# Stick-breaking by summation by parts in a one-layer decoder trunk, and four rearrangements around it

## The chip, the core and the metric

The kernel runs on one core of a Trainium2 chip. Times are device microseconds of one execution. Five engines each work through a list of instructions of their own in order: TensorE (PE; its weight loads, PEld, overlap the matmuls), VectorE (DVE), ScalarE (ACT), GpSimd (POOL) and SyncE (SP, which only issues DMAs; ACT and POOL issue some too). An instruction that waits for a semaphore holds up all that stands behind it on its engine.

## What is computed

One layer of a hybrid trunk on 1024 tokens of width 1024 in fp32. One projection `h @ w_in` feeds three branches and their gates: an RWKV-7 recurrence (8 heads of 64), stick-breaking attention (8 heads of 64) and cross-attention to 256 memory tokens. The gated branches are summed, projected and added to x, and a convolutional feed-forward network follows. The part that the change rewrites is this:

```python
z = jnp.einsum('bhqd,bhkd->bhqk', qb, kb).astype(jnp.float32) * scale
mask = s_idx[None, :] < t_idx[:, None]
log_1mb = jnp.where(mask, jax.nn.log_sigmoid(-z), 0.0)
log_between = lax.cumsum(log_1mb, axis=3, reverse=True) - log_1mb
attn = jnp.where(mask, jnp.exp(jax.nn.log_sigmoid(z) + log_between), 0.0)
outs.append(jnp.einsum('bhqk,bhkd->bhqd', attn.astype(v.dtype), vb))
```

With `sn = sigmoid(-z)` (1 where masked) and the suffix products `P[s] = sn[s] * sn[s+1] * ... * sn[W-1]`, `P[W] = 1`, a weight is `attn[s] = sigmoid(z[s]) * P[s+1]`. Since `sigmoid(z) = 1 - sn`, that is also `P[s+1] - P[s]`, and the sum over s can be taken by parts: `sum attn[s] v[s] = v[W-1] + sum P[s] (v[s-1] - v[s])`, with `v[-1] = 0`.

## The kernel before

Every fp32 matmul operand is split into a high and a low part; a product is three matmuls, high by high, high by low and low by high. `split_w` (L84) loads a 512 KB weight tile on SP's queue into one of two "wr" buffers, copies the high part on ScalarE (L80) and subtracts on GpSimd (L81). `proj_item` (L664) is a projection: 8 k-steps of six matmuls of 512 columns, 48 in all, each k-step followed by a yield; `gate_item` (L703) is one for a gate, which is then multiplied by the row norm, passed through a sigmoid and stored to `gsd` or kept.

Work is woven by hand. `run` (L1668) makes a list `items` of such generators; `stream` starts the next one, which issues its weight load and split, before it runs the present one. `weave(main, filler, ratio)` advances a main generator and, after each of its yields, the filler `pump` by `ratio` yields on average. `pump` also advances the generator `inverse` by `pace` tenths of a step per yield. Matmuls, transposes and some VectorE instructions are pinned to program order; other instructions, DMAs included, are ordered by a scheduler when the program is built, from its own estimate of when they are ready.

In order of time:

- The items project r, k and v of the recurrence, woven with `rwkv_prep` (L308). Then come eight items of `sb_v` (L615): the value projection of stick-breaking in two groups (jg) of four, 24 matmuls an item. In the fourth item of a group ScalarE copies the four results, scaled, into `self.v` (L643), four tiles of [128 keys, 2 x 512] that the attention reads later.
- `rwkv_prep` writes each head's 64 x 64 chunk matrices to `mad`, and GpSimd loads them into `inst`, one matrix per partition. `inverse` (L459) inverts all 128 in place: 62 pairs of a product and an addition on VectorE (L466, L468), 124 steps, and then sixteen DMAs on GpSimd's queue to `td` (L475).
- `sb_attn` (L785) runs 64 units (pair of heads, half, head, block of 128 queries), with gates, memory projections and inverse steps as filler. `front` makes z in PSUM and two sigmoids, `sn` (L806) and `sp` (L807); `weigh` a reversed scan of products over `sn` (L813) and a multiply into `sp` (L814); `mid` transposes `sp` (L105, by way of L824) and copies it back from PSUM into the tile of `sn` (L825); `back` multiplies it by `self.v` and copies the sum into the one "ys" buffer (L845), from where ScalarE's queue stores it to `yd` (L848). These tiles are "at" tiles, of which there are seven. In program order a unit's `mid` comes two units after its `front`, its `back` four.
- `mem_attn` (L1001) does cross-attention; `back` copies y into the "ys" buffer (L1050) and stores it (L1051).
- `ld1` loads the stick-breaking result of `yd` (L1082) and splits it on ScalarE (L1073) and VectorE (L1074); the high part, `yhi`, takes the buffer of `inst`. The products with `w_br` follow in `branch_item` (L1090), as filler of `stage2` (L477), the recurrence over 16 chunks. Its loads are made in `load` (L490): chunk matrices `scr` (L493), values `vd` (L497) and inverses `td` (L498). Then come `group_norm` (L588), the last branch, the output projection and the feed-forward network.

`need(name)` advances the filler until an item has set that mark.

Of the kernel before, what the change touches and what calls it, by code (L numbers as in the profile page):

```python
# [22 lines left out]
NG = NC // 2  # L23
# [26 lines left out]
class Trunk:  # L50
# [408 lines left out]
    def inverse(self):  # L459
# [11 lines left out]
        for p in range(4):  # L471
            for h2 in range(2):
                for cc in range(2):
                    i0 = p * 32 + h2 * 16 + cc
                    nc.gpsimd.dma_start(self.td[p // 2, :, h2, :, p % 2, cc * 64 : cc * 64 + 64], X[i0 : i0 + 15 : 2])  # L475

    def stage2(self):  # L477
# [12 lines left out]
        def load(g, p, what="LV"):  # L490
# [3 lines left out]
            if "V" in what and p % 2 == 0:  # L494
# [3 lines left out]
                nc.sync.dma_start(V2[:, 512:768], self.td[p // 2, g].rearrange("h s p i -> (h s) (p i)"))  # L498
# [116 lines left out]
    def sb_v(self):  # L615
        nc = self.nc
        out = {}
        self.v = []

        def item(jg, kt):  # L620
# [4 lines left out]
            if (jg, kt) == (0, 3):  # L625
                self.v += [self.t4("A", n=1024) for _ in range(4)]

# [7 lines left out]
            for i in range(4):  # L635
# [5 lines left out]
                if kt == 3:  # L641
                    jj = jg * 4 + i
                    nc.scalar.activation(self.v[jj // 2][:, (jj % 2) * 512 : (jj % 2 + 1) * 512], out[jg][i], AF.Copy, scale=self.rsc[:, jj : jj + 1])  # L643
# [4 lines left out]
        return [item(jg, kt) for jg in range(2) for kt in range(4)]  # L648

    def head_norm(self, pst, nh, width, fold, neg=None):  # L650
# [8 lines left out]
        if neg is not None:  # L659
            nc.gpsimd.tensor_tensor(v3(neg), v3(f), b3(self.rscn), ALU.mult)  # L660
        nc.gpsimd.tensor_tensor(v3(f), v3(f), b3(self.rsc), ALU.mult)
# [61 lines left out]
    def sb_qk(self, p, out):  # L723
# [40 lines left out]
        def q_split(i):  # L764
# [7 lines left out]
            if i == 1:  # L772
                out.extend((st["S"], *st["K"], *st["f"]))

        def q_ss():
            nf = self.small("nf", [128, 16])
            f = self.head_norm(self.head_ss(st["q"][0]), 2, SBD, SBD ** -0.5, nf)
            st["f"] = f, nf
# [6 lines left out]
    def sb_attn(self, qk, need):  # L785
# [4 lines left out]
        def front(u):  # L790
            p, half, h2, b = units[u]
            need(f"sb{p}")
            S, K, KL, f, nf = qk[p]
            W = (b + 1) * 128
            ts = slice(b * 128, (b + 1) * 128)
            sn, sp = self.t4("at", n=1024), self.t4("at", n=1024)
            for w0 in range(0, W, 512):
# [9 lines left out]
                nc.scalar.activation(sp[:, w0:w1], pz[:, : w1 - w0], AF.Sigmoid, scale=f[:, i : i + 1])  # L807
            st[u] = (sn, sp)

        def weigh(u):  # L810
            W = (units[u][3] + 1) * 128
            sn, sp = st[u]
            self.pinned(nc.vector.tensor_tensor_scan(sn[:, :W][:, ::-1], sn[:, :W][:, ::-1], sp[:, :W], 1.0, ALU.mult, ALU.bypass))  # L813
            self.pinned(nc.vector.tensor_tensor(sp[:, : W - 1], sp[:, : W - 1], sn[:, 1:W], ALU.mult))  # L814

        def mid(u):
            b = units[u][3]
            W = (b + 1) * 128
            at, sp = st[u]
            for w0 in range(0, W, 512):  # L820
                w1 = min(w0 + 512, W)
                pt = self.ps("g")
                for o in range(w0, w1, 128):
                    self.transpose(pt[:, o - w0 : o - w0 + 128], sp[:, o : o + 128])  # L824
                nc.scalar.activation(at[:, w0:w1], pt[:, : w1 - w0], AF.Copy)  # L825

        def back(u):
            p, half, h2, b = units[u]
            ats = [st.pop(u + i)[0] for i in range(2)]
# [171 lines left out]
    def mem_attn(self, mq, need):  # L1001
# [666 lines left out]
    def run(self):  # L1668
# [36 lines left out]
        items += [lambda: drain(inv), ld1, gate(), mark("y1"), *br1, ld2, gate(), *br2]  # L1705
# [22 lines left out]
        pace[0] = 5  # L1728
        self.weave(self.sb_attn(qk, need), pump, 1.03, 0)
        pace[0] = 5  # L1730
# [6 lines left out]
        self.weave(st2, pump, 2.25, 0)  # L1737
# [82 lines left out]
```

## Time and profile before

| | us |
|---|---|
| three timed runs | 1930.93, 1934.08, 1934.30 (median 1934.08) |
| the profiled execution | 1926.05 |
| its span, first to last instruction | 1924.3 |
| mean granted TensorE clock in it | 0.985 |

The stages touched by the change lie in it as follows: value projection of stick-breaking about 240 to 287 us, stick-breaking attention 340 to 680, memory attention to about 818, start of branch 1 and of the recurrence 818 to 860, recurrence and branch products to about 1100. From 1311 on TensorE is all but full.

How to read the rows: in a table of stages each engine's busy time stands in us with its count of instructions, then the granted clock, the mean busy share of the 16 DMA engines, and GB/s. In a list of waits a row gives who waited, for whom, the sum in us, how often, and the longest. In a timeline a row is start, length, engine, line, operation, output <- input, and in brackets the idle time just before it and what ended it. A group row ends with count, busy us, mean ns, and the idle time before it. A DMA row gives count, size, and the median us from issue to landing.

### The profile page before, as it was taken

Reading aid. Unit: us, or ns where it says so; the run is one execution under the profiler, and the core shown is the slowest. Engines: PE = TensorE matmul, PEld = TensorE weight load, DVE = VectorE, ACT = ScalarE, POOL = GpSimd, SP = SyncE. Lnnn points to the kernel's source line nnn. Section 1 sums busy time; section 2 is a strip of 40 time slices with the busy share of each in tenths; the row PEclk is TensorE's granted clock in tenths of the full one; section 3 lists DMA queues with packets and bytes.
Section 4 is the critical chain, followed back from the end, with each engine's and each line's share of the span. In section 5 each row is a group of like instructions: output and inputs, shape, how many; then the busy total and the mean of one; then the engine's idle time right before and its main releaser. Section 6 shows DMA issues by size and latency. Waiting matters only on the chain. (4 is left out here: it accounts for less than half of the span.)

```text
span 1924.3 us, 27682 instructions
## 1 busy us (share of the span) xinstructions
PE 1834.8 (95%) x10500; PEld 1455.7 (76%) x10500; DVE 1230.2 (64%) x1702; ACT 922.4 (48%) x1729; POOL 791.7 (41%) x451
## 2 busy tenths in 40 slices
PE   8999999999998999979999989989999999999999
PEld 6777778777776787757777867767888888878877
DVE  5756666888888855223433475267777767785486
ACT  5444343667576635425445433354444444445433
POOL 2223252222221342412233353357767676645444
PEclk9999999999999999979999999999999999999999
DMA  4255662111111331577534464222333223376465
GB/s 173 68 163 165 186 192 71 61 39 50 39 53 61 99 96 50 142 237 265 184 133 175 143 220 137 92 99 93 97 107 111 97 86 117 116 283 239 141 228 192
DMA packets 117268, 254.99 MB, mean 133 GB/s; under 512 B 28048, under 2 KB 40592, under 8 KB 117008
## 3 DMA queue, kind: packets, MB, share of 16 engines
q1 hardware_dynamic: 81040, 190.54, 30.1%
q10 hardware_dynamic: 32320, 50.08, 7.5%
q0 software_dynamic: 3776, 12.62, 2.4%
q8 instruction: 82, 1.34, 0.3%
q14 instruction: 50, 0.41, 0.1%
HBM read 175.83 MB, written 77.33 MB: 132 GB/s over the span
## 5 line engine op out<-in xcount | busy, mean ns | idle before, releaser
L81 POOL TENSOR_TENSOR wl<-wr,wh 128x1024 fp32r<-128x1024 f32 x77 | 200.7, 2607 | 542.4 <-ACT wh L80 526.7
L112 PE MATMUL mm<-xhi,wh 128*128 128x512 f32 x784 | 270.1, 425 | 8.6 <-ACT xhi L184 7.6
L112 PE MATMUL mm<-xlo,wh 128*128 128x512 f32 x784 | 249.4, 399 | 0.8 <-DVE xlo L185 0.8
L112 PE MATMUL mm<-xhi,wl 128*128 128x512 f32 x784 | 248.0, 398 | 0.4 <-POOL wl L81 0.4
L112 PEld LDWEIGHTS mm<-xlo,wh 128*128 128x128 f32 x784 | 149.4, 191 | 37.4 <-DVE xlo L185 1.5
L112 PEld LDWEIGHTS mm<-xhi,wl 128*128 128x128 f32 x784 | 148.6, 190 | 37.0 <-POOL wl L81 0.8
L112 PEld LDWEIGHTS mm<-xhi,wh 128*128 128x128 f32 x784 | 137.5, 192 | 40.7 <-issue 8.2
L80 ACT ACTIVATE wh<-wr 128x1024 fp32r<-128x1024 f32 x77 | 81.7, 1062 | 139.1 <-PE mm L112 87.4
L112 PE MATMUL mm<-dw,da 128*128 128x512 f32 x528 | 121.3, 390 | 1.5 <-DVE da L1563 1.4
L112 PE MATMUL mm<-BT,l 128*128 128x512 f32 x504 | 119.9, 393 | 0.0
L813 DVE TENSOR_TENSOR_SCAN at<-at,at 128x128 f32<-128x128 f32 (+3 forms) x64 | 97.2, 1518 | 30.6 <-ACT at L807 30.4
L112 PEld LDWEIGHTS mm<-dw,da 128*128 128x128 f32 x528 | 98.9, 188 | 23.3 <-DVE da L1563 2.3
L1564 POOL TENSOR_TENSOR dw<-draw,dw 128x512 fp32r<-128x512 f32 x55 | 80.2, 1465 | 85.9 <-ACT dw L1562 85.8
L112 PE MATMUL mm<-BT,wh 128*128 128x512 f32 x352 | 109.9, 393 | 3.5 <-DVE u L1376 3.5
L112 PE MATMUL mm<-B,wh 128*128 128x512 f32 x352 | 110.4, 395 | 1.6 <-ACT p L1418 1.6
L112 PEld LDWEIGHTS mm<-BT,l 128*128 128x128 f32 x504 | 94.6, 188 | 22.0
L1563 DVE TENSOR_TENSOR da<-draw,da 128x512 fp32r<-128x512 f32 x77 | 64.6, 848 | 62.4 <-ACT da L1561 61.9
L112 PE MATMUL g<-dw,da 128*128 128x512 f32 x396 | 92.4, 394 | 2.4 <-ACT dw L1562 1.3
L1324 POOL TENSOR_TENSOR l<-it,l 128x1024 fp32r<-128x1024 f32 x21 | 50.6, 2410 | 100.5 <-ACT l L1323 100.5
L112 PEld LDWEIGHTS g<-dw,da 128*128 128x128 f32 x396 | 75.4, 191 | 18.9 <-ACT dw L1562 1.7
L1561 ACT ACTIVATE da<-draw 128x512 fp32r<-128x512 f32 x77 | 48.3, 629 | 84.3 <-PE mm L112 40.9
L112 PEld LDWEIGHTS mm<-BT,wh 128*128 128x128 f32 x352 | 65.9, 188 | 19.7 <-DVE u L1376 4.3
(321 smaller groups left out, 4132.4 us busy)
## 6 DMA issues: line engine op xcount, KB each, us to landing
wr<-in_w_in_dram SPq DMA_DIRECT2D x50, 512.0 KB, 3.6
draw<-actd SPq DMA_DIRECT2D x77, 256.0 KB, 4.0
at<-scr SPq DMA_DIRECT2D x32, 512.0 KB, 6.0
draw<-in_w_down_dram SPq DMA_DIRECT2D x55, 256.0 KB, 4.9
wr<-in_w_up_dram SPq DMA_DIRECT2D x22, 512.0 KB, 3.6
actd<-gall ACTq DMA_DIRECT2D x44, 256.0 KB, 2.9
rw<-in_w_up_dram SPq DMA_DIRECT2D x20, 512.0 KB, 3.6
actd<-gall ACTq DMA_DIRECT2D x11, 768.0 KB, 3.8
```

The costliest lines, as they stand in the source:

```text
L80: self.nc.scalar.activation(hi, raw, AF.Copy)
L81: self.nc.gpsimd.tensor_tensor(lo, raw, hi.bitcast(F32), ALU.subtract)
L112: self.pinned(self.nc.tensor.matmul(*a, **k))
L813: self.pinned(nc.vector.tensor_tensor_scan(sn[:, :W][:, ::-1], sn[:, :W][:, ::-1], sp[:, :W], 1.0, ALU.mult, ALU.bypass))
L1324: nc.gpsimd.tensor_tensor(lo, src, hi.bitcast(F32), ALU.subtract)
L1561: self.pinned(nc.scalar.activation(A[:, 0], a, AF.Copy))
L1563: self.pinned(nc.vector.tensor_tensor(A[:, 1], a, A[:, 0].bitcast(F32), ALU.subtract))
L1564: nc.gpsimd.tensor_tensor(Wt[:, 1], w, Wt[:, 0].bitcast(F32), ALU.subtract)
```

## The change

1. Stick-breaking by parts. `weigh` is only the scan (its unused second operand is now `self.rbc`); there is no `sp`, no second sigmoid and no multiply. `mid` transposes the scanned `sn` into an "at" tile that it takes itself. `sb_v` makes differences: ScalarE copies into `raw`, DMAs write `raw` one row down into `self.v`, the boundary rows come from the last row of the tile before, and VectorE subtracts. The last value row of each 128-key block goes through the new DRAM tile `vld` into `vlast` (eight DMAs) and is added as the bias of ScalarE's copy of y, which therefore is four instructions instead of two.
2. `head_norm` gives back only the negated factor.
3. The inverse keeps pace 8 from the first stick-breaking unit on, and is stored in one DMA of its own layout; `stage2` loads its four pieces by four DMAs in place of one.
4. Memory attention's y is written into the first half of its own weight tile pT; the "ys" buffer is not used there.
5. Gates 0 and 1 of branch 2 are projected after `ld1`, before the first product of branch 1, and stored to `gsd`; they are loaded again in branch 2. The ratio of the filler of `stage2` goes from 2.25 to 2.08.

```diff
-        self.td = self.pool_d.tile([2, NG, 2, 64, 2, 128], F32, name="td")
+        self.td = self.pool_d.tile([128, 64, 64], F32, name="td")
...
+        self.vld = self.pool_d.tile([4, 1024], F32, name="vld")
...
-        for p in range(4):
-            for h2 in range(2):
-                for cc in range(2):
-                    i0 = p * 32 + h2 * 16 + cc
-                    nc.gpsimd.dma_start(self.td[p // 2, :, h2, :, p % 2, cc * 64 : cc * 64 + 64], X[i0 : i0 + 15 : 2])
+        nc.gpsimd.dma_start(self.td, X)
...
-                nc.sync.dma_start(V2[:, 512:768], self.td[p // 2, g].rearrange("h s p i -> (h s) (p i)"))
+                td = self.td.rearrange("(p h g c) s i -> p h g s c i", p=4, h=2, g=NG)
+                for i, h2 in heads[0:4]:
+                    nc.sync.dma_start(V2[hq[h2], 512 + i * 128 : 640 + i * 128].rearrange("s (c i) -> s c i", c=2), td[p + i, h2, g])
...
+        halves = [slice(0, 512), slice(512, 1024)]
+
+        def differ(i, raw):
+            v = self.v[i]
+            nc.sync.dma_start(v[1:128], raw[0:127])
+            nc.sync.dma_start(v[0:1, halves[1]], raw[127:128, halves[0]])
+            if i < 3:
+                nc.sync.dma_start(self.v[i + 1][0:1, halves[0]], raw[127:128, halves[1]])
+            nc.sync.dma_start(self.vld[i : i + 1], raw[127:128])
+            nc.vector.tensor_tensor(v, v, raw, ALU.subtract)
...
+                nc.vector.memset(self.v[0][0:1, halves[0]], 0.0)
...
-                    nc.scalar.activation(self.v[jj // 2][:, (jj % 2) * 512 : (jj % 2 + 1) * 512], out[jg][i], AF.Copy, scale=self.rsc[:, jj : jj + 1])
+                    if i % 2 == 0:
+                        raw = self.t4()
+                    nc.scalar.activation(raw[:, (jj % 2) * 512 : (jj % 2 + 1) * 512], out[jg][i], AF.Copy, scale=self.rsc[:, jj : jj + 1])
+                    if i % 2:
+                        differ(jj // 2, raw)
...
+    def load_vlast(self):
+        self.vlast = self.small("jk", [128, 64], bufs=1)[:, :32].rearrange("c (i u) -> c i u", i=4)
+        for i in range(4):
+            for e in range(2):
+                self.nc.sync.dma_start(
+                    self.vlast[e * 64 : e * 64 + 64, i], self.vld[i, e * 512 : e * 512 + 512].rearrange("(u c) -> c u", c=64))
...
             nc.gpsimd.tensor_tensor(v3(neg), v3(f), b3(self.rscn), ALU.mult)
+            return neg
...
-            sn, sp = self.t4("at", n=1024), self.t4("at", n=1024)
+            sn = self.t4("at", n=1024)
...
-                nc.scalar.activation(sp[:, w0:w1], pz[:, : w1 - w0], AF.Sigmoid, scale=f[:, i : i + 1])
-            st[u] = (sn, sp)
+            st[u] = sn
...
-            self.pinned(nc.vector.tensor_tensor_scan(sn[:, :W][:, ::-1], sn[:, :W][:, ::-1], sp[:, :W], 1.0, ALU.mult, ALU.bypass))
-            self.pinned(nc.vector.tensor_tensor(sp[:, : W - 1], sp[:, : W - 1], sn[:, 1:W], ALU.mult))
+            self.pinned(nc.vector.tensor_tensor_scan(sn[:, :W][:, ::-1], sn[:, :W][:, ::-1], self.rbc[:, :W], 1.0, ALU.mult, ALU.bypass))
...
-            at, sp = st[u]
+            at, sn = self.t4("at"), st[u]
+            st[u] = at
...
-                    nc.scalar.activation(
-                        y[q].rearrange("c (b i t) -> c b i t", b=2, i=2)[:, :, i],
-                        py[i * 64 : i * 64 + 64, 0:256].rearrange("c (b t) -> c b t", b=2), AF.Copy)
+                    rows = slice(i * 64, i * 64 + 64)
+                    for bb in range(2):
+                        o = (2 * bb + i) * 128
+                        nc.scalar.activation(
+                            y[q, o : o + 128], py[rows, bb * 128 : bb * 128 + 128], AF.Identity,
+                            bias=self.vlast[rows, half * 2 + bb, 2 * p + h2 : 2 * p + h2 + 1])
...
-            y = self.t4("ys", n=512)
+            y = pT[:, 0:512]
...
+        gq[14:14] = [(2, 0), (2, 1)]
...
+            if p == 0:
+                items.append(self.load_vlast)
...
-        items += [lambda: drain(inv), ld1, gate(), mark("y1"), *br1, ld2, gate(), *br2]
+        items += [lambda: drain(inv), ld1, gate(), gate(), gate(), mark("y1"), *br1, ld2, gate(), *br2]
...
-        pace[0] = 5
         self.weave(self.sb_attn(qk, need), pump, 1.03, 0)
-        pace[0] = 5
...
-        self.weave(st2, pump, 2.25, 0)
+        self.weave(st2, pump, 2.08, 0)
```

More of the change, by code (lines that the diff above doesn't have):

```diff
@@ L772, in q_split @@
             if i == 1:
-                out.extend((st["S"], *st["K"], *st["f"]))
+                out.extend((st["S"], *st["K"], st["f"]))
         def q_ss():
             nf = self.small("nf", [128, 16])
-            f = self.head_norm(self.head_ss(st["q"][0]), 2, SBD, SBD ** -0.5, nf)
-            st["f"] = f, nf
+            st["f"] = self.head_norm(self.head_ss(st["q"][0]), 2, SBD, SBD ** -0.5, nf)
         w = self.I["w_in"]
@@ L792, in front @@
             need(f"sb{p}")
-            S, K, KL, f, nf = qk[p]
+            S, K, KL, nf = qk[p]
             W = (b + 1) * 128
             ts = slice(b * 128, (b + 1) * 128)
-            sn, sp = self.t4("at", n=1024), self.t4("at", n=1024)
+            sn = self.t4("at", n=1024)
             for w0 in range(0, W, 512):
@@ L806, in front @@
                 nc.scalar.activation(sn[:, w0:w1], pz[:, : w1 - w0], AF.Sigmoid, scale=nf[:, i : i + 1])
-                nc.scalar.activation(sp[:, w0:w1], pz[:, : w1 - w0], AF.Sigmoid, scale=f[:, i : i + 1])
-            st[u] = (sn, sp)
+            st[u] = sn
         def weigh(u):
             W = (units[u][3] + 1) * 128
-            sn, sp = st[u]
-            self.pinned(nc.vector.tensor_tensor_scan(sn[:, :W][:, ::-1], sn[:, :W][:, ::-1], sp[:, :W], 1.0, ALU.mult, ALU.bypass))
-            self.pinned(nc.vector.tensor_tensor(sp[:, : W - 1], sp[:, : W - 1], sn[:, 1:W], ALU.mult))
+            sn = st[u]
+            self.pinned(nc.vector.tensor_tensor_scan(sn[:, :W][:, ::-1], sn[:, :W][:, ::-1], self.rbc[:, :W], 1.0, ALU.mult, ALU.bypass))
         def mid(u):
@@ L823, in mid @@
                 for o in range(w0, w1, 128):
-                    self.transpose(pt[:, o - w0 : o - w0 + 128], sp[:, o : o + 128])
+                    self.transpose(pt[:, o - w0 : o - w0 + 128], sn[:, o : o + 128])
                 nc.scalar.activation(at[:, w0:w1], pt[:, : w1 - w0], AF.Copy)
@@ L828, in back @@
             p, half, h2, b = units[u]
-            ats = [st.pop(u + i)[0] for i in range(2)]
+            ats = [st.pop(u + i) for i in range(2)]
             if b % 4 == 0:
```

## Prediction

> **What bounds the kernel now.** I read the busy table first, then a table of busy time by stage, then who waits for whom on TensorE, then the timeline of single engines where TensorE stands still.
>
> ```profile
> span 1924.3 us, 27682 instructions
> PE 1834.8 (95%) x10500; PEld 1455.7 (76%) x10500; DVE 1230.2 (64%) x1702; ACT 922.4 (48%) x1729; POOL 791.7 (41%) x451
> ```
>
> TensorE is busy for 1834.8 of 1924.3 us. The change neither adds nor removes a matmul, so it can gain only out of the 89 us in which TensorE is idle and out of slow clock after idle stretches. The stages show where these lie (columns: window, length, then busy time of PE, PEld, DVE, ACT, POOL, granted clock, DMA share, GB/s):
>
> ```profile
> 240.00:300.00 60.00, 59.04 (x333) 45.82 (x332) 33.56 (x40) 23.07 (x31) 28.47 (x12) 1.00 0.60 176
> ...
> 340.00:680.00 340.00, 316.89 (x2157) 251.28 (x2157) 289.29 (x257) 223.70 (x415) 86.14 (x38) 0.98 0.19 59
> 680.00:818.00 138.00, 136.46 (x824) 108.81 (x824) 59.10 (x128) 64.57 (x135) 47.06 (x36) 1.00 0.35 95
> 818.00:860.00 42.00, 27.88 (x170) 20.18 (x169) 12.02 (x21) 12.26 (x26) 6.40 (x6) 0.76 0.68 229
> 860.00:905.00 45.00, 42.50 (x428) 32.99 (x426) 14.16 (x41) 17.46 (x66) 8.03 (x8) 0.96 0.82 277
> 905.00:1100.00 195.00, 186.85 (x1688) 146.53 (x1687) 80.38 (x202) 98.04 (x346) 61.19 (x31) 0.98 0.47 160
> ```
>
> Two stages matter. Stick-breaking attention (340 to 680) leaves TensorE idle for 340 - 316.9 = 23.1 us, with VectorE at 289 of 340 us; the granted clock of 0.98 costs up to another 0.02 x 340 = 6.8 us. The start of the recurrence and of branch 1's products (818 to 860) has 42 - 27.9 = 14.1 us idle at a clock of 0.76. By contrast the stage of the value projection (240 to 300) has almost nothing to give, 1.0 us, and much to lose. The waits of TensorE:
>
> ```profile
> PE mm L112 <- ACT yhi L1073: 12.7, 2, 9.5
> PE g L105 <- DVE at L814: 12.1, 6, 4.1
> ...
> PE mm L112 <- DVE w L1111: 5.0, 1, 5.0
> ...
> PE g L105 <- ACT at L825: 4.7, 4, 1.8
> ...
> PE g L105 <- ACT at L807: 2.6, 3, 1.0
> ```
>
> The first belongs to 818-860, the third to the group norm near 1118; the other three are stick-breaking transposes that wait for the weights (multiply L814, transpose copy L825, sigmoid L807).
>
> **The hole at 818 us: gain.** What stands before it on POOL, ACT and TensorE:
>
> ```profile
> 795.07 6.47 POOL L475 DMA_DIRECT2D td<-inst  x8 [8.39 <-DVE inst L468]
> ...
> 813.91 1.69 POOL L475 DMA_DIRECT2D td<-inst  x2 [1.47 <-DMA td<-inst]
> 812.79 0.60 ACT L1050 ACTIVATE ys<-mm 128x512 f32<-128x512 f32 x1 [7.13 <-DMA yd<-ys]
> ...
> 824.91 0.60 ACT L1050 ACTIVATE ys<-mm 128x512 f32<-128x512 f32 x1 [9.14 <-DMA yd<-ys]
> ...
> 826.95 1.99 ACT L1073 ACTIVATE yhi<-w 128x1024 fp32r<-128x1024 f32 x2
> 828.05 1.22 PE L112 MATMUL mm<-yhi,wh 128*128 128x512 f32 x2 [9.47 <-ACT yhi L1073]
> ...
> 834.21 1.06 PE L112 MATMUL mm<-yhi,wl 128*128 128x512 f32 x2
> 835.06 1.06 PE L112 MATMUL mm<-yhi,wh 128*128 128x512 f32 x2
> ...
> 856.27 0.62 PE L112 MATMUL mm<-yhi,wh 128*128 128x512 f32 x2
> 856.72 0.62 PE L112 MATMUL mm<-A,wh 128*128 128x512 f32 x2
> ```
>
> The inverse ends at 795 (its last step releases POOL), and its sixteen stores fill POOL and the DMA engines until 815. Meanwhile memory attention's stores of y crawl, and since there is one ys buffer ScalarE stands 7.13 and 9.14 us in front of y, with the split of the loaded branch input (yhi) queued behind it. TensorE has one gate of cover left, then waits 9.47 us, and runs at half speed afterwards: two matmuls start 0.85 us apart (834.21, 835.06), later 0.45 (856.27, 856.72). From 828 to 847 that costs about 15 pairs x 0.40 = 6 us. The hole is worth 14.1 + 6 = 20 us.
>
> All three of its causes go. The inverse runs at pace 8 through stick-breaking instead of 5: about 79 of its 124 steps fall into that stage now (the row of L466 below, and as many additions), 8/5 of them would be 126, so it and its store end before 680, beside work with a DMA share of 0.19. There is one store of 2 MB; the nearest row for its shape, `inst<-mad`, lands 512 KB in 6.6 us, so about 4 x 6.6 = 26 us at worst, and nobody waits for it before 800:
>
> ```profile
> inst<-mad POOLq DMA_DIRECT2D x4, 512.0 KB, 6.6
> ...
> yd<-ys ACTq DMA_DIRECT2D x16, 128.0 KB, 2.2
> ...
> scr<-qk SPq DMA_DIRECT2D x8, 512.0 KB, 3.7
> ...
> td<-inst POOLq DMA_DIRECT2D x16, 128.0 KB, 11.1
> qk<-td SPq DMA_DIRECT2D x16, 128.0 KB, 5.1
> ```
>
> Memory attention's y goes into half of pT, so the ys wait goes; pT is held some 2 us longer out of seven buffers. And two more gates lie between the loads and the products: 48 matmuls each at 0.23 us (half of 0.45) are 22 us of cover for a wait of 9.5. They are taken from branch 2, so the work is only moved. I take the whole 20 us; the bounds are 14 (only idle time) and 20.
>
> **Stick-breaking: gain.** Rows by line, stage 325 to 680:
>
> ```profile
> L813 DVE TENSOR_TENSOR_SCAN at<-at,at 128x128 f32<-128x128 f32 (+3 forms) x64 | 97.2, 1518 | 30.6 <-ACT at L807 30.4
> ...
> L814 DVE TENSOR_TENSOR at<-at,at 128x127 f32<-128x127 f32 (+3 forms) x64 | 60.9, 952 | 5.2
> L807 ACT ACTIVATE at<-g,hf 128x512 f32<-128x512 f32 (+2 forms) x96 | 55.9, 584 | 0.5 <-POOL hf L661 0.5
> ...
> L466 DVE TENSOR_TENSOR it<-inst 128x720 f32<-128x720 f32 (+21 forms) x39 | 49.6, 1271 | 0.3
> ```
>
> Removed: 64 multiplies (60.9 us of VectorE), 96 sigmoids (55.9 us of ScalarE), one of two "at" tiles between front and mid. The scan keeps its length; `rbc` as unused second operand lies in SBUF as `sp` did. Added: 32 copies of y become 64 short ones (at least 0.28 us each, about 6 us more ScalarE), and the faster pace: about 22 inverse steps that now run after 680, of some 0.7 us, so 16 us, come into the stage, and while they last the rate of inverse steps per unit is 8/5. Net VectorE 289 - 61 + 16 = 244 us, but per unit, while the inverse runs, the multiply's 0.95 us is nearly given back by 0.85 us of more inverse. The chain of a unit is shorter in any case: sigmoid, scan, transpose. Out of 23.1 + 6.8 = 30 us I take 20; the bounds are 8 (only the half of the 12.1 us that VectorE's queue does not take back, and its clock) and 28.
>
> **The value differences: loss.** Each of four value tiles is now copied out to `raw`, moved down one partition by a DMA of 127 rows of 4 KB, topped with two single rows, stored one row wide, and subtracted on VectorE (four of about 1.2 us, hidden at 34 of 60 us busy). The two pairs are issued when the copies out of PSUM are done, and the weights of the later items are on the same SP queue:
>
> ```profile
> 252.41 1.90 ACT L643 ACTIVATE A<-mm,rsc 128x512 f32<-128x512 f32 x3 [3.02 <-PE g L105]
> 261.19 0.33 SPq L76 DMA_DIRECT2D wr<-in_w_v_dram  x1
> 262.34 1.16 PE L112 MATMUL g<-qk,qk 64*128 64x128 f32 x16
> ...
> 277.90 0.50 PE L112 MATMUL mm<-wh,xhi 128*128 128x512 f32 x1
> ...
> 286.75 0.69 ACT L643 ACTIVATE A<-mm,rsc 128x512 f32<-128x512 f32 x1
> ```
>
> No DMA here has 127 rows; the price has two ends. If it spreads over 16 engines like `scr<-qk`, 512 KB in 3.7 us, it costs nothing. If one engine takes all rows in turn, each costs what a 4 KB packet costs an engine in a saturated stretch (1130 to 1140):
>
> ```profile
> q1 hardware_dynamic: 934, 3.44, 89.7%
> ```
>
> 0.897 x 16 x 10 us / 934 = 0.154 us, so 127 rows take 19.5 us and a pair 39. I take the second end: `td<-inst`, with 8 rows outermost, needs 11.1 us for 128 KB where `yd<-ys`, with 64 rows, needs 2.2 (part of the 11.1 is queueing behind its fifteen neighbours). The Trainium skill, "DMA: Bandwidth & Descriptors", section on why a DMA increments its semaphore by 16, says the same more sharply: the engines used are the largest number up to 16 that divides the outer size, so 127 partitions go to one; by it both pairs cost what follows, and no run here shows it yet.
>
> First pair: issued at 254.3, done at 295. The weights of the last value item, issued at 261.19, have their share behind it; after ScalarE's split (1.1 us) TensorE starts at about 297 instead of 277.90. That is 19 us, and 3 us of half clock after it. Second pair: last copy at 286.75 + 0.69 + 19 = 307, done at 347. Its victim is the fourth projection after the value items, reached three projections of 11.2 us and some head sums later, near 342, so 5 us. Loss 19 + 3 + 5 = 27; bounds 0 and, with VectorE caught as well (below), 50.
>
> **Small parts.** The eight column loads of the last values (4 B pieces, 512 each) go out beside a DMA share of 0.19, a unit before use; a queue delay of a few us is covered by the next item's weights being one item early. The recurrence loads T in 64 DMAs of 32 KB instead of 16 of 128 KB that land in 5.1: 48 more issues of about 0.5 us on SP and pieces a quarter as long, at a share of 0.82 to 905. Nothing but the next group's loads is queued behind them; I charge 2 us, bounds 0 and 6. The filler of the recurrence falls from 137 to 121 yields and its rate from 2.25 to 2.08, so it ends seven yields earlier in the group norm, where TensorE waits 5.0 us already; I put this at 0, bounds -3 and +5.
>
> **Sum.** The profiled execution took 1926.05 us, span 1924.3 and 1.75 around it. 1926 - 20 - 20 + 27 + 2 = 1915. The three timed runs have their median 8 us higher, at 1934.08; the same -11 gives 1923.
>
> **Rivals.** *Spread copies*: the 127 rows use all engines; loss 0 instead of 27, so 1923 - 27 = 1896. For it: every 512 KB transfer of the profile lands in 3 to 7 us. Against: all of those have row counts that 16 divides. *Slower, through VectorE's order*: the four subtractions stand in VectorE's queue where a quick copy was assumed. If it stands there until 295, the attention preparation behind it stops, and with it TensorE at the products of 262.34 instead of at 277.90: 33 us instead of 19, though some of the work behind is done between the two copies. At the second pair the head norm of the first k waits until 347 and needs some 12 us more, 17 us instead of 5. Loss 50 with the clock; if the inverse's pace also leaves the stick-breaking gain at 10, the time is 1934 - 20 - 10 + 50 + 2 = 1956. It decides when VectorE is held more than 10 us at one subtraction. *Not what it says*: the inverse at pace 8 takes back all of VectorE's gain, stick-breaking stays at 23 us idle and the first pair alone is late: 1934 - 20 + 22 = 1936.
>
> **Chances.** Forecast 0.42 (1910 to 1938, most of it faster), spread copies 0.25, VectorE's order 0.26, not what it says 0.07. A measurement of this kernel tells 0.2%, 4 us, from no change. Faster: 0.27 of the forecast and all 0.25 of the spread, 0.52; slower: 0.07 + 0.26 + 0.03 = 0.36; same 0.12. The range from 1890 to 1956 leaves out the ends of the two outer cases.
>
> **What will show it.** Right: no ScalarE wait for yd and no TensorE gap over 3 us at the start of branch 1; stick-breaking idle near 8 us; a gap of about 19 us in the value items with a late weight load. Wrong: shift copies landing in 5 us (then 1896), or VectorE idle before the subtractions for tens of us (then 1950s), or stick-breaking idle still above 18 us.

## The result and the profile after

| | before | after |
|---|---|---|
| median of four runs, us | 1934.19 (1930.93 to 1936.22) | 1965.22 (1960.79 to 1970.50) |
| the profiled execution, its span | 1926.05, 1924.3 | 1968.17, 1966.4 |
| mean granted TensorE clock in it | 0.985 | 0.972 |

The change made the kernel slower: ratio 1.0163, 95% interval 1.0131 to 1.0196. The forecast was 1923 (1890 to 1956). The head of the page after the change, busy time of each engine:

```profile
span 1966.4 us, 27535 instructions
PE 1836.3 (93%) x10500; PEld 1458.2 (74%) x10500; DVE 1167.1 (59%) x1643; ACT 886.9 (45%) x1665; POOL 775.3 (39%) x432
```

TensorE does the same 1836 us of work but stands idle for 130 us instead of 89. To see where, I divided both executions at three instructions that both have: the first and the last of the 64 scans of stick-breaking, and the last store of x2 ahead of the feed-forward part. These are the rows of the changed kernel (count, shortest/median/longest ns, first and last start):

```profile
L833 DVE TENSOR_TENSOR_SCAN at<-at,rbc x64: 410/1351/4474, 412.2 to 723.1; 128x128 f32<-128x128 f32 x8, 128x256 f32<-128x256 f32 x8, 128x384 f32<-128x384 f32 x8, 128x512 f32<-128x512 f32 x8
L1226 ACTq DMA_DIRECT2D x2d<-w x8: 326/326/327, 1227.2 to 1304.0; - x8
```

and those of the kernel before:

```profile
L813 DVE TENSOR_TENSOR_SCAN at<-at,at x64: 414/1478/4483, 340.5 to 669.0; 128x128 f32<-128x128 f32 x8, 128x256 f32<-128x256 f32 x8, 128x384 f32<-128x384 f32 x8, 128x512 f32<-128x512 f32 x8
L1203 ACTq DMA_DIRECT2D x2d<-w x8: 326/326/327, 1188.7 to 1265.6; - x8
```

The differences of these starts give four stages, which all runs below are read by:

| stage, us | before | after | difference |
|---|---|---|---|
| start to first scan | 340.5 | 412.2 | +71.7 |
| stick-breaking, first to last scan | 328.5 | 310.9 | -17.6 |
| last scan to last store of x2 | 596.6 | 580.9 | -15.7 |
| from there to the end | 658.7 | 662.4 | +3.7 |

The sum, +42.1, is the difference of the two spans. Stick-breaking and the stretch with the hole gained about what was forecast; the whole miss lies before the first scan. There the table of stages says (columns as in the prediction's):

```profile
260.00:280.00 20.00, 9.80 (x64) 7.05 (x62) 11.66 (x13) 2.10 (x2) 4.68 (x2) 0.82 0.27 100
280.00:300.00 20.00, 7.97 (x32) 6.48 (x32) 0.59 (x2) 1.19 (x2) 1.90 (x1) 0.76 0.16 57
300.00:320.00 20.00, 8.83 (x40) 6.55 (x41) 4.54 (x7) 2.80 (x3) 4.67 (x2) 0.50 0.60 176
...
340.00:360.00 20.00, 7.41 (x32) 5.61 (x30) 1.23 (x1) 0.00 (x0) 0.00 (x0) 0.78 0.18 57
```

There are two holes, 260 to 320 and from 340 on. In both all engines stand idle for long stretches, and the granted clock goes down to 0.50. In such a stretch one looks at the DMA. From 340 to 350 the queue of SP shows:

```profile
q1 hardware_dynamic: 67, 0.26, 6.4%
...
A<-w SPq DMA_DIRECT2D x1, 2.0 KB, 34.0
```

6.4% of sixteen engines is one engine busy all the time: 0.064 x 160 us / 67 packets = 0.153 us for a row of 4 KB. The shift copies do run on one engine, as the prediction took it, and a single row of 2 KB behind them takes 34.0 us from issue to landing. What waits for them, first on VectorE, ScalarE and TensorE:

```profile
278.08 1.23 DVE L627 TENSOR_TENSOR A<-A,w 128x1024 f32<-128x1024 f32 x1 [8.23 <-issue]
301.14 1.23 DVE L627 TENSOR_TENSOR A<-A,w 128x1024 f32<-128x1024 f32 x1 [20.55 <-DMA A<-w]
...
370.88 1.23 DVE L627 TENSOR_TENSOR A<-A,w 128x1024 f32<-128x1024 f32 x1 [20.43 <-DMA A<-w]
```

```profile
311.52 1.06 ACT L80 ACTIVATE wh<-wr 128x1024 fp32r<-128x1024 f32 x1 [28.95 <-DMA wr<-in_w_v_dram]
...
372.05 1.06 ACT L80 ACTIVATE wh<-wr 128x1024 fp32r<-128x1024 f32 x1 [34.96 <-DMA wr<-in_w_in_dram]
```

```profile
PE g L112 <- ACT w L754: 26.7, 1, 26.7
PE g L112 <- DVE at L401: 15.0, 1, 15.0
PE g L105 <- DVE at L401: 14.1, 3, 10.2
...
PE mm L112 <- ACT wh L80: 6.9, 1, 6.9
```

In the first hole TensorE waits 10.2 and 15.0 us for VectorE's mask multiplies (L401), which stand behind the subtractions, and then 6.9 us for weights; in the second 26.7 us for ScalarE, whose list stands at a split of late weights. Why are the weights late? On SP's own timeline the length of a DMA instruction is the time SP needs to issue it:

```profile
253.60 0.72 SPq L622 DMA_DIRECT2D A<-w  x1
254.41 8.92 SPq L625 DMA_DIRECT2D A<-w  x1
...
269.74 1.31 SPq L622 DMA_DIRECT2D A<-w  x1
271.10 15.31 SPq L623 DMA_DIRECT2D A<-w  x1
...
306.21 0.68 SPq L76 DMA_DIRECT2D wr<-in_w_v_dram  x1
...
323.38 12.13 SPq L625 DMA_DIRECT2D A<-w  x1
...
336.77 18.42 SPq L623 DMA_DIRECT2D A<-w  x1
```

A 127-row copy (L622) is issued in 0.6 to 1.3 us, but the single rows behind it take 8.92, 15.31, 12.13 and 18.42 us to issue; before the change the issue of one DMA in this stretch took about 0.3 to 1.0 us. VectorE does not make these stands: it works without a gap from 251 to 269.85, while the first of them ends at 263.33. The load of the last value weights goes out at 306.21, where it went out at 261.19 before. Of this delay VectorE has a part, since between 290 and 304 SP also waits 10.7 us for mask multiplies (L401) whose result it stores; how much that counts is shown by a run below (e13).

At branch 1 the hole is gone: no wait for a y buffer stands before the split, and TensorE is busy throughout from 840 to 900.

```profile
862.03 1.99 ACT L1096 ACTIVATE yhi<-w 128x1024 fp32r<-128x1024 f32 x2
```

```profile
840.00:860.00 20.00, 20.00 (x91) 14.66 (x90) 5.76 (x11) 12.69 (x24) 2.50 (x2) 1.00 0.64 224
860.00:880.00 20.00, 20.00 (x84) 15.51 (x83) 7.99 (x6) 9.60 (x11) 2.40 (x1) 1.00 0.71 259
880.00:900.00 20.00, 20.00 (x90) 15.93 (x90) 5.38 (x3) 6.19 (x8) 4.80 (x2) 1.00 0.45 151
```

### The profile page after: what moved, and what is told of

It reads as the page before. It is cut to its first block, busy times and chain, and to the rows that moved or that the text cites. A ratio compares the mean times of both kernels' runs of the same rounds, so it can differ in the third digit from the quotient of the medians.

```text
span 1966.4 us, 27535 instructions
## 1 busy us (share of the span) xinstructions
PE 1836.3 (93%) x10500; PEld 1458.2 (74%) x10500; DVE 1167.1 (59%) x1643; ACT 886.9 (45%) x1665; POOL 775.3 (39%) x432
## 5 line engine op out<-in xcount | busy, mean ns | idle before, releaser
L81 POOL TENSOR_TENSOR wl<-wr,wh 128x1024 fp32r<-128x1024 f32 x77 | 194.6, 2528 | 616.2 <-ACT wh L80 593.9
L833 DVE TENSOR_TENSOR_SCAN at<-at,rbc 128x128 f32<-128x128 f32 (+3 forms) x64 | 91.2, 1426 | 45.2 <-ACT at L827 45.1
L112 PE MATMUL g<-qk,qk 64*128 64x128 f32 (+2 forms) x448 | 69.6, 329 | 16.6 <-DVE at L401 15.0
```

Of the source, the lines that this page charges most:

```text
L81: self.nc.gpsimd.tensor_tensor(lo, raw, hi.bitcast(F32), ALU.subtract)
L112: self.pinned(self.nc.tensor.matmul(*a, **k))
```

## The experiments

Three questions: is it the one engine, and by which rule of rows; does its backlog act through VectorE or through SP; and which of the other edits earned the 33 us. Each result is given with its ratio to the kernel before, run beside it, and the 95% interval of that ratio.

### Is it the row count?

**e1_split112** and **e17_126_1**: the copy in two pieces, on the same queue.

```diff
-            nc.sync.dma_start(v[1:128], raw[0:127])
+            nc.sync.dma_start(v[1:113], raw[0:112])
+            nc.sync.dma_start(v[113:128], raw[112:127])
```

```diff
+            nc.sync.dma_start(v[1:127], raw[0:126])
+            nc.sync.dma_start(v[127:128], raw[126:127])
```

> The changed kernel, with each shift copy cut in two: rows 0 to 111 and rows 112 to 126. Nothing else differs. Theory (the 127-row copies run on one DMA engine, row after row, and hold both SP at the issues behind them and VectorE at the subtraction): 112 rows spread over 16 engines and 15 rows over 15, each lands in 3 to 8 us, SP's single-row issues take under 2 us each, the first scan comes near 345 us instead of 412, and the time is 1885 to 1905. Rival (the loss lies in the extra work of the differences or in stick-breaking's new form, not in how the rows are spread): the time stays above 1945. By the Trainium skill, page DMA: Bandwidth & Descriptors, section Why a DMA increments its semaphore by 16 and not by 1, 112 rows use 16 engines and 15 rows use 15.

> The changed kernel with each shift copy cut into 126 rows and one row. Theory (the largest number up to 16 that divides the rows gives the engines): 126 rows go to 14 engines, nine rows each, and land in 3 to 8 us; the time is that of 112 and 15 rows, 1896 to 1912. Rival (rows that are no multiple of 16 all go to one engine): nothing changes, 1950 to 1972. By the Trainium skill, page DMA: Bandwidth & Descriptors, section Why a DMA increments its semaphore by 16 and not by 1, it is the first.

Measured: 1905.65 (0.9865, 0.9834 to 0.9896) and 1910.86 (0.9885, 0.9858 to 0.9913). The 112 rows, 448 KB, land in 4.4 us, and no issue of a row takes SP over 2 us:

```profile
A<-w SPq DMA_DIRECT2D x4, 448.0 KB, 4.4
```

One more DMA a tile, for one or fifteen of the 127 rows, turns a kernel 1.6% slower into one 1.1 to 1.4% faster. Since 126 rows are about as good as 112 (the intervals overlap), it is not that 16 has to divide the rows. The Trainium skill, "DMA: Bandwidth & Descriptors", section "Why a DMA increments its semaphore by 16 and not by 1", says that the engines used on these queues are the largest number up to 16 that divides the slowest dimension. 127 is prime, and the runs agree. Not all of the loss is gone: the first scan comes at 354.3 and 355.0 us, 14 behind the kernel before.

**e2_poolqueue**: the same 127 rows from GpSimd's queue.

```diff
-            nc.sync.dma_start(v[1:128], raw[0:127])
+            nc.gpsimd.dma_start(v[1:128], raw[0:127])
```

> The changed kernel, with the four 127-row copies issued from GpSimd's queue instead of SP's; size and rows are the same. Tells the two ways apart by which one engine's backlog costs 72 us before the first scan. Theory A (SP stands at the issues behind a shift copy, and the weight loads behind SP are late): SP's single-row issues take under 2 us, weights come on time, and only the subtraction's wait is left: 1910 to 1935. Theory B (VectorE stands at the subtraction, with the mask and norm work behind it): the copies still land in 20 us or more, VectorE waits as before, and the time stays above 1945. If the copies land in under 8 us from this queue, then the one-engine spread belongs to SP's queue, and the time is 1885 to 1905.

Measured: 1899.08 (0.9816, 0.9775 to 0.9858), first scan at 349.2, and the third outcome of the expectation: from this queue 127 rows spread.

```profile
A<-w POOLq DMA_DIRECT2D x4, 508.0 KB, 6.5
```

The same section of the Trainium skill names this exception: for some direct copies GpSimd's queue shares 127 partitions out over all sixteen engines. 6.5 us for what takes some 19.5 row by row agrees. But the run took away VectorE's wait and SP's stand together, so it does not tell them apart. Its four executions lie further apart than most, from 1892.69 to 1907.02, and the profiled one is the slowest of them; differences from this run of under about 10 us are uncertain.

**e6_all_pool**: the single rows and the stores of last values from GpSimd's queue too (all of `differ`).

> As the run with the 127 rows on GpSimd's queue, with the single rows and the stores of the last value rows there too, so that SP has none of the differences' transfers. Theory (what is left of the loss there, first scan at 349 us against 340 before, comes from SP waiting for ScalarE's copy at the single rows, with a weight load behind): first scan at 340 to 344, time 1890 to 1896. Rival (it comes from the extra work on VectorE and GpSimd): first scan at 347 to 352, time 1896 to 1905.

Measured: 1903.26 (0.9858, 0.9838 to 0.9878), first scan at 348.2. The theory missed: with none of these transfers on SP the first scan is still 8 us late, so what is left is not SP's wait at the single rows. The trace shows TensorE waiting 3.0 us at 264 for a low part from GpSimd, and a granted clock of 0.83 from 260 to 280, where the kernel before has no such wait and a clock of 1.00; that this makes the 8 us was not tried.

### VectorE or SP?

**e3_sub_on_pool**: the subtraction on GpSimd. **e5_actqueue**: the 127 rows from ScalarE's queue.

```diff
-            nc.vector.tensor_tensor(v, v, raw, ALU.subtract)
+            nc.gpsimd.tensor_tensor(v, v, raw, ALU.subtract)
```

```diff
-            nc.sync.dma_start(v[1:128], raw[0:127])
+            nc.scalar.dma_start(v[1:128], raw[0:127])
```

> The changed kernel, with the four subtractions on GpSimd instead of VectorE; the copies and their queue stay. Theory A (SP's issue sets the loss): the gap stays, 1945 to 1970. Theory B (VectorE's order sets it): VectorE no longer waits for the copies, and the first scan comes 30 to 50 us earlier, 1915 to 1940; GpSimd's low parts of the weights, which then stand behind the subtraction, take some of that back. Both at once: between the two.

> The changed kernel, with the four 127-row copies issued from ScalarE's queue; the single rows stay on SP. From GpSimd's queue the same copies landed in 6.5 us and the time was 1899, which took away the one-engine spread and SP's stand together. Here they come apart if ScalarE's queue spreads 127 rows as SP's does. Theory A (SP's stand at the issues behind a shift copy was the loss): the copies land in 20 to 40 us and VectorE waits for them as before, but SP's single-row issues take under 2 us, weights are on time, and the time is 1905 to 1930. Theory B (VectorE's wait at the subtraction is the loss): 1945 to 1970. If the copies land in under 8 us here, it was SP's queue alone that did not spread them, and the time is 1890 to 1905.

Measured: 1961.61 (1.0152, 1.0120 to 1.0183) and 1961.45 (1.0168, 1.0148 to 1.0188): both as slow as the change. In the first VectorE is free, but GpSimd holds a weight's low part behind its subtraction (TensorE waits 11.8 us for it), and the late loads still cost one wait of 18.1 and another of 26.3:

```profile
PE mm L112 <- ACT wh L80: 18.1, 1, 18.1
PE mm L112 <- POOL wl L81: 13.0, 2, 11.8
```

In the second ScalarE's queue does not spread the rows either (from 335 to 345 us the DMA engines are busy for 0.07 of the time, about one of sixteen). VectorE waits as before, SP's single rows go out in 0.5 to 2.5 us, and now ScalarE is the one that stands at its own issues, with its splits behind:

```profile
282.69 7.15 ACTq L438 DMA_DIRECT2D ggd<-qk  x1
289.96 1.06 ACT L80 ACTIVATE wh<-wr 128x1024 fp32r<-128x1024 f32 x1 [22.05 <-issue]
```

So the stand goes with the queue. Neither run shows what freeing one engine is worth, since GpSimd took VectorE's place in the first and ScalarE took SP's in the second. But in the second the last value weights are split by 291 us, and TensorE still waits 13.2 and 12.5 us for VectorE's multiplies, until 306: VectorE's order alone would fill most of the first hole.

**e9_first_pair**, **e10_second_pair**: one pair of copies on SP's queue, the other on GpSimd's.

```diff
-            nc.sync.dma_start(v[1:128], raw[0:127])
+            (nc.sync if i < 2 else nc.gpsimd).dma_start(v[1:128], raw[0:127])
```

> The 127-row copies of the first two value tiles on SP's queue, as in the changed kernel; those of the last two on GpSimd's, where they landed in 6 us. In the changed kernel the last product of the value projection comes 39 us late (323.7 against 284.6) and the first scan 72, so the first pair should cost about 39 less what GpSimd's queue also costs, the second about 33. Theory (the two pairs add up): 1930 to 1940. Rival (only the second pair's late weight loads count, the first is caught up): under 1915. Prediction's sizes: 22 us over the run with all four on GpSimd's queue, 1921.

> The reverse: the first two copies on GpSimd's queue, the last two on SP's. VectorE's head norm of the first k waits at two subtractions, and SP stands at the rows behind the copies, with a weight load of the projections behind it. Theory (the pairs add up): 1925 to 1935, with a TensorE gap of 20 to 30 us at the first head sums. Prediction's size for the second pair, 5 us (17 by the rival of VectorE's order): 1904, or 1916.

Measured: 1936.82 (1.0021, 1.0002 to 1.0040) and 1939.11 (1.0024, 1.0006 to 1.0042). Beside the run with all four on GpSimd's queue the first pair costs 38 us and the second 40, where the prediction had 22 and 5. Both together cost 66 there (1965.22 - 1899.08), so some of it overlaps; e10 alone lies above the 1935 of its theory. In the second pair's run TensorE waits 14.0 us for ScalarE and 21.0 us for VectorE, and both go back to VectorE's subtractions (L627):

```profile
PE g L105 <- DVE w L259: 21.0, 1, 21.0
PE g L112 <- ACT w L754: 14.0, 1, 14.0
```

```profile
323.16 1.06 ACT L754 ACTIVATE w<-w 128x1024 f32<-128x1024 f32 x1 [22.45 <-DVE A L627]
344.05 1.06 ACT L80 ACTIVATE wh<-wr 128x1024 fp32r<-128x1024 f32 x1 [19.84 <-DMA wr<-in_w_in_dram]
```

```profile
342.79 1.23 DVE L627 TENSOR_TENSOR A<-A,w 128x1024 f32<-128x1024 f32 x1 [19.72 <-DMA A<-w]
```

ScalarE's square of k (L754), a tile of the same pool as `raw`, stands 22.45 us until the first subtraction is done; the head norm of k (L259) stands in VectorE's list behind the second. The weights behind SP's stand are split at 344, when that subtraction ends too. So here the list names VectorE, and no run takes VectorE out for the second pair alone.

**e13_late_sub**: e9 with the first pair's subtractions behind the mask multiplies in VectorE's list.

```diff
-            nc.vector.tensor_tensor(v, v, raw, ALU.subtract)
+            sub = lambda: self.pinned(nc.vector.tensor_tensor(v, v, raw, ALU.subtract))
+            late.append(sub) if i < 2 else sub()
...
+                    while jg == 1 and late:
+                        late.pop(0)()
```

> As the run with the first pair's 127 rows on SP's queue and the second pair's on GpSimd's (1937), with the first pair's subtractions moved down VectorE's list, behind the mask multiplies (L401 there) that TensorE waits for. The copies and SP's list of the shift rows stay. Theory A (VectorE's order makes the first pair's loss): TensorE's waits of 10.3 and 15.1 us for those multiplies go, the first scan comes 20 to 30 us earlier than 380, time 1907 to 1918. Theory B (SP's stand makes it, since the weights of the last value items are behind it anyway): the waits move to the weights, first scan at 370 or later, time above 1925.

Measured: 1932.59 (0.9993, 0.9980 to 1.0006), first scan at 378.6 against 380.4 in e9. For the first pair this is the run that tells. TensorE's waits between 240 and 345 us in e9:

```profile
PE g L112 <- DVE at L401: 15.1, 1, 15.1
PE g L105 <- DVE at L401: 10.3, 1, 10.3
PE mm L112 <- ACT wh L80: 6.8, 1, 6.8
```

and in e13, followed by SP's issues there:

```profile
PE mm L112 <- ACT wh L80: 31.0, 1, 31.0
```

```profile
269.03 1.35 SPq L623 DMA_DIRECT2D A<-w  x1
270.49 15.21 SPq L285 DMA_DIRECT2D scr<-qk  x1
...
286.56 8.02 SPq L405 DMA_DIRECT2D scr<-at  x1
...
303.28 0.36 SPq L76 DMA_DIRECT2D wr<-in_w_v_dram  x1
```

15.1 + 10.3 + 6.8 = 32.2 us of waits for VectorE and then for weights become one wait of 31.0 for weights, which SP issues at 303.28 instead of 304.79. VectorE's wait was the one that the list of waits named; with VectorE freed, SP's stand alone makes the first hole as long.

### What the other edits earned

**e4_no_parts**: the kernel before with points 3, 4 and 5 of the change alone. **e16_one_store**: the kernel before with the new layout of T alone (one store, 64 loads).

> The kernel before with points 3, 4 and 5 of the change alone: inverse at pace 8 stored in one DMA and loaded in 64, memory attention's y in pT, two gates moved, ratio 2.08. No value differences, no summation by parts. Theory (the hole at 818 us is filled for 20 us, the loads of T cost 2): 1934 - 20 + 2 = 1916, with VectorE busier in stick-breaking by the faster inverse, up to 1924. Rival (the hole is filled but the recurrence's loads or the group norm give it back): 1928 to 1940, with TensorE waiting for the loads of scr between 900 and 1000 us as in the changed kernel.

> The kernel before with the layout of T alone changed: one store of 2 MB, 64 loads of 32 KB. Pace, gates, y buffer and the stick-breaking form stay. On top of the summation by parts the sixteen stores cost 20 us (1904 against 1884). Theory (the sixteen stores made the hole): no ScalarE wait for y's stores, 1934 - 20 = 1914, 1908 to 1920. Rival (here the inverse ends at 795 us, 30 us later than there, and the branch has one gate of cover, so that the one store still delays the branch's split): 1922 to 1934.

Measured: 1927.03 (0.9970, 0.9954 to 0.9986) and 1922.49 (0.9950, 0.9932 to 0.9968). One edit of the group earns as much as all three. By stages, stick-breaking and from there to the last store of x2: 340.3 and 578.1 in e4, 328.7 and 584.6 in e16, 328.5 and 596.6 before. So pace 8 costs the old stick-breaking about 12 us, where the inverse and the multiply share VectorE; the 6.5 us less in the stage after are of the pace, the moved gates and y in pT together. Neither reaches its theory's time; e16 lies in its rival's range, but the late split that the rival names is not there. In e16 the store is issued at 795.82 as before, and no wait for yhi is left, although the ys buffer is (its waits are 3.6 us at most); but 5.2 us come back as a wait for the recurrence's load of scr, at 859:

```profile
859.01 0.48 PE L112 MATMUL g<-it,at 64*64 64x64 f32 x4 [5.21 <-DMA at<-scr]
```

**e8_pace5**, **e7_old_td**: e2 with the inverse at pace 5 throughout, and e2 with T stored in sixteen DMAs and loaded in 16.

```diff
+        pace[0] = 5
         self.weave(self.sb_attn(qk, need), pump, 1.03, 0)
+        pace[0] = 5
```

> As the run with the 127 rows on GpSimd's queue, with the inverse back at pace 5 from the first stick-breaking unit. Theory (the faster pace costs VectorE time where it is short, and buys that the store of T does not collide with memory attention's stores and the loads of branch 1): stick-breaking gets 5 to 12 us shorter, but the store of T comes near 790 us and the start of the recurrence waits for it; the sum is 0 to 15 us slower, 1899 to 1914. Rival (with y in pT, one store and three gates of cover the hole stays filled without the pace): 3 to 10 us faster, 1889 to 1896.

> As the run with the 127 rows on GpSimd's queue, with the inverse stored as before the change, in sixteen DMAs, and loaded in 16 instead of 64. Theory (with the inverse done near 630 us the store is hidden either way, and 48 fewer issues on SP let the loads of scr come earlier): 0 to 6 us faster, 1893 to 1899, with TensorE's wait for scr under 5 us instead of 10.6. Rival (the store is what matters): the sixteen stores hold GpSimd for some 20 us in stick-breaking and cost 5 us or more, above 1904. Second rival (neither matters): within 4 us of 1899.

Measured: 1889.93 (0.9792, 0.9777 to 0.9808) and 1911.59 (0.9908, 0.9882 to 0.9933). At pace 5 stick-breaking takes 300.6 us instead of 311.1, and the next stage no longer (581.1, 582.1), as the rival of e8 had it; the two times' intervals overlap, but nothing speaks for the faster pace on this form. The sixteen stores cost 12 us by the medians even at 630 to 649 us (the profiled executions, of which e2's is its slowest, differ by 2.6): GpSimd is held, TensorE waits 8.0 us for a low part that GpSimd makes, and stick-breaking takes 318.3 us instead of 311.1. The stage after gains 5 us (577.1 against 582.1) with 48 fewer loads: TensorE's waits for scr, 10.6 us in e2, are gone.

**e11_gates_back**, **e12_ys_back**, **e14_td16_pace5**: e8 with the two gates back in branch 2 (ratio 2.25); e8 with the ys buffer; e11 with the sixteen stores and 16 loads.

> As the run at pace 5 (copies on GpSimd's queue, 1890), with the two gates of branch 2 back in branch 2 and the ratio of the recurrence's filler at 2.25. With the inverse stored at 763 us in one DMA and y in pT, the collision that emptied TensorE at branch 1 should be gone without the gates. Theory (the gates are spare cover): within 4 us of 1890. Rival (the loads of branch 1 and their splits still take longer than one gate): 5 to 12 us slower, 1895 to 1902, with TensorE waiting for yhi.

> As the run at pace 5 (1890), with memory attention's y in the one ys buffer as before the change. Theory (ScalarE's wait of 7 and 9 us for the stores of y came from the collision with sixteen stores of T, which is gone): within 4 us of 1890. Rival (the one buffer holds ScalarE for some us at each of the eight stores): 5 us or more slower.

> As the run at pace 5 with the gates back in branch 2 (1884), with the inverse stored in sixteen DMAs and loaded in 16, as before the change. What is left of the change is then the summation by parts with copies that spread, and y in pT. Theory (the hole came from the sixteen stores falling on memory attention's end; with the inverse done at 763 us instead of 795 they fall earlier and still cost GpSimd 20 us, but the branch's loads start after them): 3 to 10 us slower, 1887 to 1894. Rival (fewer loads of T pay more than the stores cost): 1878 to 1883. Second rival (the hole is back): above 1897, with TensorE waiting 8 us or more for yhi.

Measured: 1884.24 (0.9763, 0.9738 to 0.9788), 1890.25 (0.9787, 0.9764 to 0.9810), 1904.47 (0.9846, 0.9824 to 0.9867). Neither the moved gates nor y in pT is worth anything here (without the moved gates it is 5.7 us less, with overlapping intervals). With the sixteen stores the hole is back, at a price of 20 us, the second rival of e14's expectation, although the inverse is done 30 us earlier than in the kernel before and there is no ys buffer to wait for:

```profile
802.80 2.00 ACT L1098 ACTIVATE yhi<-w 128x1024 fp32r<-128x1024 f32 x2 [6.59 <-DMA td<-inst]
```

The stores are issued from 765 to 790. The high part of the branch's input takes the buffer of `inst`, so it waits for the last of them, and TensorE for it (13.2 us in two waits).

e11 is the best version: summation by parts with the shift copies on GpSimd's queue, T in one store, pace 5, gates where they were. It is 48 us faster than the kernel before and 81 faster than the change. Beside e16, which has the one store and the old form of stick-breaking, that leaves 36 us by the ratios (0.9950 and 0.9763) to the summation by parts.

## Why the prediction was wrong

- **The value differences: the step that failed.** Forecast 27, measured 71.7. The copies were sized well: 0.154 us a row forecast, 0.153 measured. What failed is the sentence "The weights of the last value item, issued at 261.19, have their share behind it". It kept the time of issue from the trace of before and let only the transfer be late. In fact SP stands at its next issues while that engine works off its rows, so the load was issued at 306.21, and everything else on SP with it; e13 shows that this is enough for the whole first hole. The first pair cost 38 us instead of 22.
- **The second pair, 40 us instead of 5.** The prediction had only "the fourth projection after the value items" late. In the changed kernel the stands at 323 and 337 put the loads of the next projections behind them, and TensorE waits 26.7 us at a split of late weights; with VectorE free (e3) it is still 26.3. In the run of the second pair alone (e10) its waits of 14.0 and 21.0 us go back to VectorE's subtractions. Which of the two makes the 40 us stays open.
- **The rival through VectorE's order** had the sign, and its time, 1956, was nearest. VectorE is held over 20 us at single subtractions, as it said, and the head norm of the first k is late as it said. Its 33 us for the first pair is near the 38 measured. But with VectorE freed (e13) the first scan came only 1.8 us earlier, so that pair's loss does not need VectorE's wait: the stand alone makes it. Its 17 us for the second pair was too small, and it left stick-breaking a gain of 10 that was 17.6; that its total came so near is in part luck.
- **The spread-copies rival** (1896) is what the four kernels with spread copies and all else as in the change show, 1899 to 1911. Even then 8 to 14.5 us stay before the first scan.
- **The hole: right in size, wrong in its cause.** Forecast -20 with +2 for the loads of T, measured -15.7 for the stage. Of the three causes that the prediction named the sixteen stores are the one that counts: with one store instead the wait for yhi goes (e16), with them it returns (e14), and with one store ys and gates change nothing (e11, e12). The faster pace also takes the stores away from there (e7 has no wait for yhi), but they then cost stick-breaking time. ScalarE's 7.13 and 9.14 us at the ys buffer came with the stores: with one store and the same buffer they are 3.6 at most.
- **Stick-breaking: right.** Forecast -20 within 8 to 28, measured -17.6. That the inverse's pace takes back part of it was also right: at pace 5 the gain is 27.9 (328.5 - 300.6), at pace 8 the old form would have lost 11.8. One reading was short: in the trace of before about 28 inverse steps of 19 us run after 680, not 22 of 16.
- **Small parts.** The 48 more loads of T cost about 5 us against the forecast 2 (e7); with the two gates back in branch 2 TensorE waits only 1.1 us for scr in spite of them (e11). The last stage's +3.7 us was not in the sum. TensorE's waits for u in the up phase, 7.7 us instead of 3.5, would account for it; over all the kernels this stage, which no edit touches, lies between 658.7 and 665.5, and its cause was not tried.

## What to carry to other kernels

Before a shift by one partition is written as a DMA, look at the row count: 127 rows on SP's or ScalarE's queue go through one engine, 112 + 15 or 126 + 1 do not. Cost a slow transfer not only by who waits for its data but by what its issuing engine cannot issue meanwhile; the time of issue of everything behind it moves too. And where two waits run side by side, the profile names the later one; only a run that removes it shows whether the other was as long.

## What was not expected of the hardware

An engine that issues DMAs can be held by the issue itself: behind a 127-row copy on the same queue a single-row DMA of 2 KB took SP 18.42 us to issue, and 34.0 us passed from the start of the issue until it landed. And a hole costs twice: after TensorE's 15.0 us wait, which ended at 303, the granted clock was 0.50 over the whole stretch from 300 to 320, which holds another wait of 6.9 us and 8.83 us of work at that clock.
